# Seven block products for eight in part of the down projection of a decoder layer

## The chip, the cores and the metric

The kernel runs on one core of one Trainium2 chip. The metric is the device time of one execution in microseconds. It is given as the median of several runs; one further execution was recorded by the hardware profiler, and all views of the profile are of that one.

## The reference

One decoder layer on 256 tokens of width 1024, in float32: a combined input projection, pooling and attention heads, an output projection, cross-attention into 256 memory tokens, and a dense gated feed-forward block, each followed by a LayerNorm with a scaled residual. The change touches the last block:

```python
def swiglu(h, w_gate, w_up, w_down):
    return (jax.nn.silu(h @ w_gate) * (h @ w_up)) @ w_down
...
        h = layer_norm(DEEPNORM_ALPHA * h + swiglu(h, w_gate[l], w_up[l], w_down[l]),
                       ln3_g[l], ln3_b[l])
```

`w_gate` and `w_up` are 1024x2816, `w_down` is 2816x1024, and `DEEPNORM_ALPHA` is the fourth root of 2.

## The kernel before

Matrix products are done in a split form. Each float32 operand is kept as a high part, rounded to the format that TensorE reads (`hi`), and the remainder (`lo`). A product of two such operands is three matmuls, high by high, high by low and low by high, which `three` issues (lines 258 to 260). For a weight the high part is a cast on ScalarE (line 96) and the low part a subtraction on VectorE (line 98). `split` (lines 321 and 322) does the same for activations.

All large weights go through one `Stream` in a fixed order. It keeps 7 buffers for raw weights as they arrive by DMA on SyncE's queue (line 80) and 8 buffers each for high and low parts. A tile of the stream has 128 partitions of 1024 columns. `prepare` makes the parts of the next tiles and then fetches further raw ones. While TensorE uses tile i, the tiles up to i + 8 are prepared, each as soon as the tile eight places back has been used. Engines run their instructions in the order in which the program issues them; there is no reordering by a scheduler.

The feed-forward block has eleven chunks of 256 hidden channels (`NFC = 11`). For each chunk, `proj_both` computes gate and up in four PSUM banks: first for all eight blocks of 128 input channels the high weights against the high and low token parts side by side (32 matmuls of 512 columns, line 704), then the low weights against the high token parts (32 matmuls of 256 columns, line 710). Class `Gated` finishes a chunk during the next one: `add` joins the two halves of each bank (lines 840, 841), `multiply` applies silu and multiplies (lines 845, 846), and `split` makes the high and low parts of the gated activations, held transposed: 128 channels by 256 tokens, twice per chunk.

Down then multiplies the gated activations by `w_down`, 22 blocks of 128 rows, one tile of the stream each. A block of activations (128 channels by 128 tokens) is the stationary operand and 512 columns of weights move. `project` holds four accumulators, one for each pair of a token block and a half of the 1024 columns. It goes through the first 16 row blocks for all four. For the last 6 row blocks, which are all kept in the buffers, it goes accumulator by accumulator, the last in two pieces of 256 columns, so that the residual, the LayerNorm statistics (`Norm.add`) and the finish of a token block can begin while others are still computed. `Norm.finish`'s steps are done in `finish`: the statistics, the centring (line 618), the scaling (line 623) and the stores.

Of the kernel before, what the change touches and what calls it, by code (L numbers as in the profile page):

```python
# [8 lines left out]
F32 = mybir.dt.float32  # L9
F32R = mybir.dt.float32r  # L10
# [19 lines left out]
NEG = -3.0e38  # L30

RAW_BUFS, W_BUFS, AHEAD = 7, 8, 8
A8_BUFS = 9
PR_BUFS = 6
BUSY = 7


def r32(t):
    return t.bitcast(F32)


class Stream:


    def __init__(self, nc, pool):
        self.nc, self.pool = nc, pool
        self.src, self.raws, self.tiles, self.homes = [], [], [], []
        self.loads, self.splits = {}, {}
        self.used, self.held = 0, True
        self.pace, self.asked = 1, 0  # L50
        self.cuts, self.casts = {}, {}

    def add(self, src, parts=2):

        n = src.shape[1] // parts
        first = len(self.src)
        self.src += [src[:, i * n:(i + 1) * n, :] for i in range(parts)]
        return range(first, len(self.src))

    def before(self, number, load):  # L60

# [6 lines left out]
    def fetch(self, upto, queue):  # L68

        while len(self.raws) < min(upto, len(self.src)):  # L70
            i = len(self.raws)
            for load in self.loads.pop(i, []):
                load()
            src = self.src[i]
            if i < len(self.homes):
# [5 lines left out]
            self.raws.append(raw)  # L81

    def prepare(self, upto, eng=None):
        nc = self.nc
        while len(self.tiles) < min(upto, len(self.src)):
            i = len(self.tiles)
            src = self.src[i]
            for split in self.splits.pop(i, []):
                split()
            self.fetch(i + 1, nc.sync)  # L90
            raw = self.raws[i]
            hi = self.pool.tile(list(src.shape), F32R, tag="hi", name=f"w{i}h")
            lo = self.pool.tile(list(src.shape), F32R, tag="lo", name=f"w{i}l")
            for group in self.casts.get(i, [[slice(None)]]):
                for s in group:
                    nc.scalar.copy(hi[:, :, s], raw[:, :, s])  # L96
                s = slice(group[0].start, group[-1].stop)
                (eng or nc.vector).tensor_sub(lo[:, :, s], raw[:, :, s], r32(hi[:, :, s]))
            self.tiles.append((hi, lo))
            self.fetch(max(i + 1, len(self.homes)) + RAW_BUFS, nc.sync)  # L100

    def get(self, numbers, k):

# [24 lines left out]
def decoder_layer(  # L128
# [30 lines left out]
    def rows(w, k0, c0, nk=1, width=D):  # L159
        return ws.add(w[k0 * P:(k0 + nk) * P, c0:c0 + width].rearrange("(k p) n -> p k n", p=P), 1)  # L160
# [23 lines left out]
    c_dn = [rows(w_down, k, 0) for k in range(FB)]  # L184


    xt = ap.tile([P, T, D], F32, tag="a8", name="xt")
# [46 lines left out]
    ws.before(c_dn[4][0], load_norm("g", 3, ln3_g))  # L234
    ws.before(c_dn[6][0], load_norm("b", 3, ln3_b))

    ident = cp.tile([P, P], F32, name="ident")
    make_identity(nc, ident)
# [16 lines left out]
    def three(ps, w, y, start, stop, part=False):  # L255

        (wa, wb), (ya, yb) = w, y
        nc.tensor.matmul(ps, wa, ya, start=start, stop=False, skip_group_check=part)  # L258
        nc.tensor.matmul(ps, wa, yb, start=False, stop=False, skip_group_check=part)  # L259
        nc.tensor.matmul(ps, wb, ya, start=False, stop=stop, skip_group_check=part)  # L260

    def pair(hl, *ix):
        return hl[0][ix], hl[1][ix]
# [48 lines left out]
    def run(gen, n=None):  # L312

        while n is None or n > 0:
            if next(gen, gen) is gen:
                return False
            n = None if n is None else n - 1
        return True

    def split(h, l, ps):  # L320
        nc.scalar.copy(h, ps)  # L321
        nc.vector.tensor_sub(l, ps, r32(h))  # L322
# [265 lines left out]
    class Norm:  # L588
# [105 lines left out]
    oT = (a8("oTh", F32R), a8("oTl", F32R))  # L694
    xqT, xpr, xpt = {}, {}, {}

    def proj_both(pss, numbers, yT):

        for k in range(KD):
            hi, _ = ws.get(numbers, k)
            for b, ps in enumerate(pss):
                nc.tensor.matmul(ps, hi[:, b * P:(b + 1) * P], yT.both(k), start=k == 0, stop=False,  # L704
                                 skip_group_check=True)
            yield
        for k in range(KD):
            _, lo = ws.parts_of(numbers, k)
            for b, ps in enumerate(pss):
                nc.tensor.matmul(ps[:, S:], lo[:, b * P:(b + 1) * P], yT.pair(k)[0], start=False,  # L710
                                 stop=k == KD - 1, skip_group_check=True)
            ws.done(numbers, k)
            if not ws.held:
                ws.prepare(min(ws.used + AHEAD, len(ws.tiles) + 1))
            yield

    def do_xq(h):

# [55 lines left out]
    xattend(0)  # L774
    run(xq[3])

    h2 = ap.tile([P, T, D], F32, tag="a8", name="h2")
    xo = project(c_xo, lambda k: (oT[0][:, k], oT[1][:, k]), 4)
    xattend(1)
# [8 lines left out]
    xattend(3)  # L788


    h2T = Both("h2T")
    gT = [(a8(f"gTh{i}", F32R), a8(f"gTl{i}", F32R)) for i in range(3)]
    norm = Norm(2, h1[:, 0, :], h2[:, 0, :])
    for half in HALVES:
        norm.add(*half, until(xo)[1])
# [14 lines left out]
    run(xo)  # L810


    sg0 = sp.tile([P, T, CW], F32, name="sg", tag="pr", bufs=PR_BUFS)

    def gated_row(t, ps):
# [5 lines left out]
    def gated_t():  # L821
        pt = bank("pgt").rearrange("p (f t) -> p f t", f=2)
        for t in range(T):
            for f in range(2):
                nc.tensor.transpose(pt[:, f, t * P:(t + 1) * P], sg0[:, t, f * P:(f + 1) * P], ident)
        split(gT[0][0][:, 0:2, :], gT[0][1][:, 0:2, :], pt)

    class Gated:

# [16 lines left out]
            nc.vector.tensor_mul(gate, gate, up)  # L846
# [36 lines left out]
    pieces = PIECES[:3] + ((1, 512, 768), (1, 768, D))  # L883
    dn = project(c_dn, lambda k: (gT[k // KD][0][:, k % KD], gT[k // KD][1][:, k % KD]), 6, pieces)
    run(dn, 2)
    left.multiply()
    run(dn, 2)
    left.split()
    def finish(norm, t):
# [10 lines left out]
    norm = Norm(3, h2[:, 0, :])  # L900
    for half in HALVES:
        acc = until(dn)[1]
        for c in (0, 256):
            norm.add(half[0] + c, half[0] + c + 256, acc[:, c:c + 256])
    finish(norm, 0)

    norm = Norm(3, h2[:, 1, :])
    left = until(dn)[1]
    for c in (0, 256):
        norm.add(c, c + 256, left[:, c:c + 256])  # L910
    right = until(dn)[1]
    norm.sum(768, D, right[:, 256:])
    norm.add(512, 768, right[:, :256])
    last = until(dn)[1]
    nc.vector.tensor_add(norm.r[:, 768:], norm.r[:, 768:], last)
    norm.measure(768, D)
    finish(norm, 1)
    run(dn)
# [47 lines left out]
```

## Time and profile before

| | |
|---|---|
| median of 3 runs | 383.17 us (382.63 to 383.43) |
| profiled execution | 382.6 us, of which its span is 380.8 us |
| granted TensorE clock, mean | 0.995 |
| busy in the span: TensorE matmul | 372.1 us, 2172 instructions |
| VectorE | 262.9 us, 401 instructions |
| ScalarE | 187.8 us, 297 instructions |
| gate/up, chunks 1 to 10 | from 201.29 us, the last chunk from 301.72 us |
| down | from 312.67 us |
| last add of down's result | at 372.97 us |

The span runs from the first to the last instruction; the time of a run also holds what lies around it. A row of a timeline gives the start, the duration, the engine, the line of the kernel, the operation with what it writes and reads, and in square brackets the engine's idle time before it with what ended that. Matmuls overlap, so the step from one to the next is shorter than the duration shown.

### The profile page before, as it was taken

Reading aid. Unit: us, or ns where it says so; the run is one execution under the profiler, and the core shown is the slowest. Engines: PE = TensorE matmul, PEld = TensorE weight load, DVE = VectorE, ACT = ScalarE, POOL = GpSimd, SP = SyncE. Lnnn points to the kernel's source line nnn. Section 1 sums busy time; section 2 is a strip of 40 time slices with the busy share of each in tenths; the row PEclk is TensorE's granted clock in tenths of the full one; section 3 lists DMA queues with packets and bytes.
Section 4 is the critical chain, followed back from the end, with each engine's and each line's share of the span. In section 5 each row is a group of like instructions: output and inputs, shape, how many; then the busy total and the mean of one; then the engine's idle time right before and its main releaser. Section 6 shows DMA issues by size and latency. Waiting matters only on the chain.

```text
span 380.8 us, 5667 instructions
## 1 busy us (share of the span) xinstructions
PE 372.1 (98%) x2172; PEld 326.9 (86%) x2172; DVE 262.9 (69%) x401; ACT 187.8 (49%) x297; POOL 20.4 (5%) x31
## 2 busy tenths in 40 slices
PE   9999999999999999999999999999999999999991
PEld 9997989898888898988888888888888888888881
DVE  6768889945699758865887866666676667354265
ACT  6656677544164636544155755656544564434000
POOL 1000036200110000000100000000000000000011
PEclk9999999999999999999999999999999999999998
DMA  8996674658409953343109855546664757520011
GB/s 283 412 413 246 226 271 148 220 185 291 154 2 350 355 177 113 119 158 110 55 9 333 308 170 173 173 171 213 220 219 159 275 179 275 178 99 0 0 50 62
DMA packets 21322, 71.93 MB, mean 189 GB/s; under 512 B 2480, under 2 KB 3504, under 8 KB 21168
## 3 DMA queue, kind: packets, MB, share of 16 engines
q1 hardware_dynamic: 20720, 71.05, 53.4%
q10 hardware_dynamic: 576, 0.52, 0.4%
q8 instruction: 17, 0.28, 0.3%
q14 instruction: 9, 0.07, 0.1%
HBM read 70.52 MB, written 1.05 MB: 188 GB/s over the span
## 4 chain that ended last, share of the span: by engine, by line
PE 98%; DVE 1%; POOLq 0%; DVEq 0%; issue 0%
PE pg L704 19%; PE pg L710 10%; PE acc L258 9%; PE acc L260 9%; PE acc L259 9%; PE pqk L392 6%; PE pxk L276 6%; PE pxq L704 4%; PE pu L276 3%; PE pxq L710 2%; PE xv L258 2%; PE xv L260 2%; PE xv L259 2%; PE xs L737 2%; PE pv L258 1%; PE pg L260 1%
## 5 line engine op out<-in xcount | busy, mean ns | idle before, releaser
L613 POOL TENSOR_TENSOR rs<-rs,mhalf 128x1 f32<-128x1 f32 x6 | 6.4, 1070 | 300.4 <-DVE rs L612 300.4
L840 ACT COPY sg<-pg 128x256 f32<-128x256 f32 x40 | 12.0, 386 | 20.8 <-PE pg L710 20.8
L845 ACT ACTIVATE sg<-sg 128x512 f32<-128x512 f32 x10 | 6.3, 632 | 16.4 <-DVE sg L841 16.4
L841 DVE TENSOR_TENSOR sg<-pg,sg 128x256 f32<-128x256 f32 x40 | 14.1, 417 | 0.0
L602 DVE SCALAR_TENSOR_TENSOR r<-h,acc 128x256 f32<-128x256 f32 (+1 forms) x12 | 5.9, 501 | 10.9 <-PE acc L260 10.9
L322 DVE TENSOR_TENSOR gTl<-sg,gTh 128x512 fp32r<-128x512 f32 x10 | 6.9, 692 | 6.2 <-ACT gTh L321 6.2
L428 ACT ACTIVATE xpr<-xs,mx 128x256 f32<-128x256 f32 x8 | 3.7, 470 | 14.3 <-DVE mx L439 14.3
L428 ACT ACTIVATE pr<-pr,mx 128x128 f32<-128x128 f32 (+1 forms) x16 | 7.1, 444 | 6.8 <-DVE mx L459 6.8
L321 ACT CAST gTh<-sg 128x512 fp32r<-128x512 f32 x10 | 6.2, 620 | 7.4 <-DVE sg L846 7.4
L605 DVE BATCH_NORM_STATS2 st<-r 128x6 f32<-128x512 f32 (+1 forms) x16 | 9.0, 561 | 0.5
L321 ACT CAST h2T<-tp 128x512 fp32r<-128x512 f32 x4 | 2.4, 588 | 13.2 <-PE tp L349 13.2
L618 DVE SCALAR_TENSOR_TENSOR r<-r,mv,g 128x512 f32<-128x512 f32 (+1 forms) x10 | 8.3, 851 | 0.0
L846 DVE TENSOR_TENSOR sg<-sg 128x512 f32<-128x512 f32 x10 | 6.9, 693 | 1.0
L503 POOL TENSOR_TENSOR win<-win 128x269 f32<-128x269 f32 (+2 forms) x6 | 6.5, 1082 | 0.5
L737 PE MATMUL xs<-xkTh,xq 128*128 128x256 f32 x32 | 6.4, 282 | 0.0
L503 POOL TENSOR_TENSOR win<-upad 128x271 f32<-128x271 f32 x4 | 3.5, 871 | 53.7 <-ACT upad L531 53.7
L433 DVE RECIPROCAL sm<-sm 128x2 f32<-128x2 f32 x12 | 2.0, 166 | 6.0 <-ACT xpr L428 4.5
L623 DVE SCALAR_TENSOR_TENSOR h<-r,rs,b 128x512 f32<-128x512 f32 x8 | 5.7, 747 | 0.5 <-DVE r L618 0.5
L321 ACT CAST h1T<-tp 128x512 fp32r<-128x512 f32 x4 | 2.4, 588 | 7.1 <-PE tp L349 7.1
L737 PEld LDWEIGHTS xs<-xkTh,xq 128*128 128x128 f32 x32 | 5.2, 191 | 0.2
L349 PEld LDWEIGHTS tp<-ident,h 128*128 128x128 f32 x32 | 3.9, 141 | 1.3 <-PE pg L260 0.5
L96 ACT CAST w39h<-w39r 128x1024 fp32r<-128x1024 f32 x1 | 1.1, 1056 | 7.8 <-PE acc L260 7.8
(997 smaller groups left out, 1322.2 us busy)
## 6 DMA issues: line engine op xcount, KB each, us to landing
g<-in_ln_g SPq DMA_DIRECT2D x3, 512.0 KB, 5.0
b<-in_ln_b SPq DMA_DIRECT2D x3, 512.0 KB, 7.1
wr<-in_w_qkv SPq DMA_DIRECT2D x5, 256.0 KB, 3.9
mr<-in_mem_t SPq DMA_DIRECT2D x1, 1024.0 KB, 12.0
xt<-in_x SPq DMA_DIRECT2D x1, 1024.0 KB, 9.0
xr<-in_x_t SPq DMA_DIRECT2D x3, 256.0 KB, 5.8
wr<-in_w_qkv SPq DMA_DIRECT2D x1, 512.0 KB, 5.6
w7r<-in_w_qkv SPq DMA_DIRECT2D x1, 512.0 KB, 6.6
```

The source lines that it names most:

```text
L258: nc.tensor.matmul(ps, wa, ya, start=start, stop=False, skip_group_check=part)
L259: nc.tensor.matmul(ps, wa, yb, start=False, stop=False, skip_group_check=part)
L260: nc.tensor.matmul(ps, wb, ya, start=False, stop=stop, skip_group_check=part)
L276: nc.tensor.matmul(pss[f], w[:, s], y, start=k == 0 and f == 0 and n == 0, stop=k == KD - 1 and n == 2, skip_group_check=True)
L321: nc.scalar.copy(h, ps)
L392: nc.tensor.matmul(qk[i][:, f, :], w[:, c * P:(c + 1) * P], y, start=k == 0 and f == 0 and w is hi and y is x_hi, stop=k == KD - 1 and w i ...
L428: nc.scalar.activation(dst[:, j, :], src[:, j, :], AF.Exp, bias=mx[:, j:j + 1], scale=sign, accum_out=sm[:, j:j + 1])
L704: nc.tensor.matmul(ps, hi[:, b * P:(b + 1) * P], yT.both(k), start=k == 0, stop=False, skip_group_check=True)
L710: nc.tensor.matmul(ps[:, S:], lo[:, b * P:(b + 1) * P], yT.pair(k)[0], start=False, stop=k == KD - 1, skip_group_check=True)
L737: nc.tensor.matmul(ps[:, t, :], q[:, kk, t * P:(t + 1) * P], k[:, 2 * h + kk], start=n == 0, stop=q is q_lo and kk == 1, skip_group_check= ...
L840: nc.scalar.copy(y[:, f, :], ps[:, S:])
L841: nc.vector.tensor_add(y[:, f, :], ps[:, :S], y[:, f, :])
```

## The change

A chunk of down is a product of a matrix of 2x2 token and channel blocks (A) with a matrix of 2x2 weight blocks (B): the two token blocks by the two blocks of 128 channels, and the two blocks of 128 channels by the two halves of 512 columns. Before, this takes eight block products. For chunks 1 to 6 the change uses seven products of sums and differences of blocks (Winograd's form of Strassen's scheme), each still three matmuls of 512 columns. The remaining five chunks keep eight.

The sums of activations are formed on VectorE in `Gated.split`: four additions or subtractions of 128x128, followed by a second cast and subtraction for their high and low parts. The sums of weights are formed on VectorE in the raw buffers, in place, in `prepare_pair`. A paired chunk is three tiles of the stream instead of two: the lower row block together with one half of the upper one (which goes to a buffer of its own, `own`), then the upper buffer after it was overwritten by two differences, then the lower buffer after it was overwritten in turn. Two raw transfers serve the three.

The seven products accumulate over the six chunks in PSUM, in eight banks with the one that only unpaired chunks use. Unpaired chunks add to four of these banks. Three of the banks hold sums shared between quarters of the result. After the first eight chunks the shared banks are joined to the residual on VectorE. Then the last three chunks (8, 9 and 10, unpaired) are computed quarter by quarter as before, and each quarter is added.

The order of chunks in down becomes 1, 0, 2, 3, 4, 7, 5, 6, 8, 9, 10. In the last two chunks of gate/up, `proj_both` alternates between high and low weights in groups of two blocks instead of eight, and no tile is prepared in the last step of the last chunk. There are 11 instead of 9 large activation buffers; the room comes from a scratch area that is cut to 256 bytes.

```diff
-A8_BUFS = 9
+A8_BUFS = 11
+DOWN = (1, 0, 2, 3, 4, 7, 5, 6, 8, 9, 10)
+SEVEN = (1, 2, 3, 4, 5, 6)
+LAST = DOWN[-3:]
...
+    def prepare_pair(self, i, hi, lo):
+        nc = self.nc
+        first, step = self.pairs[i]
+        self.fetch(first + 2, nc.sync)
+        x, y = self.raws[first], self.raws[first + 1]
+        h = x.shape[2] // 2
+        (x1, x2), (y1, y2) = [(a[:, :, :h], a[:, :, h:]) for a in (x, y)]
+        sub = nc.vector.tensor_sub
+        if step == 0:
+            own = self.corner[first] = self.own(first)
+            nc.scalar.copy(own[:, 0:1, :], x1)
+            nc.scalar.copy(hi, y)
+            sub(own[:, 1:2, :], x1, r32(own[:, 0:1, :]))
+            sub(x1, x2, x1)
+            sub(x2, y2, x2)
+            sub(lo, y, r32(hi))
+        elif step == 1:
+            nc.scalar.copy(hi, x)
+            sub(y2, y2, x1)
+            sub(y1, y1, y2)
+            sub(lo, x, r32(hi))
+        else:
+            nc.scalar.copy(hi, y)
+            sub(lo, y, r32(hi))
...
+    def next(self):
+
+        if not self.held:
+            self.prepare(min(self.used + AHEAD, len(self.tiles) + 1))
...
+    def proj_both(pss, numbers, yT, group=KD):
+        for k0 in range(0, KD, group):
+            for k in range(k0, k0 + group):
+                hi, _ = ws.get(numbers, k)
...
+            for k in range(k0, k0 + group):
+                _, lo = ws.parts_of(numbers, k)
...
+                ws.done(numbers, k)
+                ws.next()
+                yield
...
         def split(self):
-            i, f = divmod(2 * self.c, KD)
-            split(gT[i][0][:, f:f + 2, :], gT[i][1][:, f:f + 2, :], self.sums[0])
+            gated_parts(self.c)
+            hi, lo = gT[self.c]
+            q = self.sums[0].rearrange("p f (t s) -> p (f t) s", t=T)
+            split(hi[:, 0:4], lo[:, 0:4], q)
+            if self.c in SEVEN:
+                a11, a21, a12, a22 = [q[:, i] for i in range(4)]
+                sums = sp.tile([P, 4, P], F32, name="sg", tag="pr", bufs=PR_BUFS)
+                s1, s2, s3, s4 = [sums[:, i] for i in range(4)]
+                nc.vector.tensor_add(s1, a21, a22)
+                nc.vector.tensor_sub(s3, a11, a21)
+                nc.vector.tensor_sub(s2, s1, a11)
+                nc.vector.tensor_sub(s4, a12, s2)
+                split(hi[:, 4:8], lo[:, 4:8], sums)
...
-        gu = proj_both(pss, c_gu[c], h2T)
+        gu = proj_both(pss, c_gu[c], h2T, KD if c < NFC - 2 else 2)
...
+        if c == NFC - 1:
+            run(gu, 2 * KD - 5)
+            ws.held = True
         run(gu)
         left = Gated(c, pss)
         left.add()
+    ws.held = False
+    ws.next()
...
+    m = {n: accbank(f"m{n}") for n in (1, 2, 3, 5)}
+    m |= {n: bank(f"m{n}") for n in (7, 6, 4, 0)}
...
+    def seven(c):
+        first = c_dn[c][0]
+        plan = (((1, 0, None), (2, 2, 0), (3, 7, 1)), ((5, 4, 0), (7, 6, 1)), ((6, 5, 1), (4, 3, 0)))
+        for i, products in enumerate(plan):
+            ws.prepare(first + i + 1)
+            hi, lo = ws.tiles[first + i]
+            for n, form, half in products:
...
+                into(n, pair(gT[c], ALL, form), w)
+                yield
+            ws.used += 1
+            ws.next()
...
+    def pieces():
+        for n, c0, c1 in ((2, 0, 512), (3, 0, 512), (4, 0, 512), (0, 0, 256), (0, 256, 512)):
...
+    dn = down()
     run(dn, 2)
     left.multiply()
-    run(dn, 2)
+    run(dn, 1)
     left.split()
+    run(dn)
+
+    lower, upper = slice(0, 512), slice(512, D)
+    norms = [Norm(3, h2[:, t, :]) for t in range(T)]
...
+    m1, u2, u3 = [shared_sum(name) for name in ("m1", "u2", "u3")]
+    nc.scalar.copy(m1, m[1])
+    with_residual(0, lower, m[1])
+    nc.vector.tensor_add(u2, m[6], m1)
+    with_residual(0, upper, m[5])
+    nc.vector.tensor_add(norms[0].r[:, upper], norms[0].r[:, upper], u2)
+    nc.vector.tensor_add(u3, m[7], u2)
+    with_residual(1, upper, m[5])
+    nc.vector.tensor_add(norms[1].r[:, upper], norms[1].r[:, upper], u3)
+    with_residual(1, lower, u3)
+    dn = pieces()
...
-    nc = bacc.Bacc("TRN2", target_bir_lowering=False, num_devices=1)
+    nc = bacc.Bacc("TRN2", target_bir_lowering=False, num_devices=1, dynamic_dma_scratch_size=256)
```

More of the change, by code (lines that the diff above doesn't have):

```diff
@@ L46, in __init__ @@
         self.nc, self.pool = nc, pool
+        self.pairs, self.corner = {}, {}
         self.src, self.raws, self.tiles, self.homes = [], [], [], []
@@ L58, in add, with add_pair @@
         return range(first, len(self.src))
+    def add_pair(self, upper, lower):
+        first = len(self.src)
+        self.src += [upper, lower, None]
+        for i in range(3):
+            self.pairs[first + i] = (first, i)
+        return range(first, first + 3)
     def before(self, number, load):
@@ L74, in fetch @@
             src = self.src[i]
+            if src is None:
+                self.raws.append(None)
+                continue
             if i < len(self.homes):
@@ L81, in fetch, with fetch_ahead @@
             self.raws.append(raw)
+    def fetch_ahead(self):
+        while len(self.raws) < len(self.src):
+            i, done = len(self.raws), len(self.tiles)
+            waiting = [j for j in range(len(self.homes), i)
+                       if self.src[j] is not None and j + (j in self.pairs) >= done]
+            if len(waiting) >= RAW_BUFS:
+                break
+            self.fetch(i + 1, self.nc.sync)
+    def prepare_pair(self, i, hi, lo):
[22 more added lines that the diff above has]
+            sub(lo, y, r32(hi))
     def prepare(self, upto, eng=None):
@@ L91, in prepare @@
             raw = self.raws[i]
-            hi = self.pool.tile(list(src.shape), F32R, tag="hi", name=f"w{i}h")
-            lo = self.pool.tile(list(src.shape), F32R, tag="lo", name=f"w{i}l")
+            shape = list((self.src[i - 1] if src is None else src).shape)
+            hi = self.pool.tile(shape, F32R, tag="hi", name=f"w{i}h")
+            lo = self.pool.tile(shape, F32R, tag="lo", name=f"w{i}l")
+            if i in self.pairs:
+                self.prepare_pair(i, hi, lo)
+                self.tiles.append((hi, lo))
+                self.fetch_ahead()
+                continue
             for group in self.casts.get(i, [[slice(None)]]):
@@ L183, in decoder_layer @@
     c_gu = [ws.add(w_gu[c], 4) for c in range(NFC)]
-    c_dn = [rows(w_down, k, 0) for k in range(FB)]
+    c_dn = {}
+    for c in DOWN:
+        tiles = [w_down[k * P:(k + 1) * P, :].rearrange("(k p) n -> p k n", p=P) for k in (2 * c, 2 * c + 1)]
+        c_dn[c] = ws.add_pair(*tiles) if c in SEVEN else [ws.add(w, 1)[0] for w in tiles]
+    ws.own = lambda i: sp.tile([P, 2, 512], F32R, tag="pair", bufs=3, name=f"w{i}c")
     xt = ap.tile([P, T, D], F32, tag="a8", name="xt")
@@ L233, in decoder_layer @@
     ws.before(c_xo[0][0], load_norm("b", 2, ln2_b))
-    ws.before(c_dn[4][0], load_norm("g", 3, ln3_g))
-    ws.before(c_dn[6][0], load_norm("b", 3, ln3_b))
+    ws.before(c_dn[DOWN[2]][0], load_norm("g", 3, ln3_g))
+    ws.before(c_dn[DOWN[3]][0], load_norm("b", 3, ln3_b))
     ident = cp.tile([P, P], F32, name="ident")
@@ L695, in decoder_layer @@
     xqT, xpr, xpt = {}, {}, {}
[L697 to L715, printed above, removed]
+    def proj_both(pss, numbers, yT, group=KD):
+        for k0 in range(0, KD, group):
+            for k in range(k0, k0 + group):
+                hi, _ = ws.get(numbers, k)
+                for b, ps in enumerate(pss):
+                    nc.tensor.matmul(ps, hi[:, b * P:(b + 1) * P], yT.both(k), start=k == 0, stop=False,
+                                     skip_group_check=True)
+                yield
+            for k in range(k0, k0 + group):
+                _, lo = ws.parts_of(numbers, k)
+                for b, ps in enumerate(pss):
+                    nc.tensor.matmul(ps[:, S:], lo[:, b * P:(b + 1) * P], yT.pair(k)[0], start=False,
+                                     stop=k == KD - 1, skip_group_check=True)
+                ws.done(numbers, k)
+                ws.next()
+                yield
     def do_xq(h):
@@ L775, in decoder_layer @@
     run(xq[3])
+    h2T = Both("h2T")
     h2 = ap.tile([P, T, D], F32, tag="a8", name="h2")
@@ L788, in decoder_layer @@
     xattend(3)
-    h2T = Both("h2T")
-    gT = [(a8(f"gTh{i}", F32R), a8(f"gTl{i}", F32R)) for i in range(3)]
     norm = Norm(2, h1[:, 0, :], h2[:, 0, :])
@@ L810, in decoder_layer, with gated_parts, gated_pair @@
     run(xo)
+    gT, shared = {}, {}
+    def gated_parts(c):
+        if c in SEVEN:
+            t = ap.tile([P, 2, 8, P], F32R, tag="a8", name=f"g{c}")
+            gT[c] = t[:, 0], t[:, 1]
+            return
+        i, j = divmod([c for c in sorted(DOWN) if c not in SEVEN].index(c), 2)
+        if j == 0:
+            shared[i] = ap.tile([P, 2, 8, P], F32R, tag="a8", name=f"go{i}")
+        gT[c] = tuple(shared[i][:, n, 4 * j:4 * j + 4] for n in range(2))
+    def gated_pair(c, k, t):
+        return pair(gT[c], ALL, 2 * k + t)
     sg0 = sp.tile([P, T, CW], F32, name="sg", tag="pr", bufs=PR_BUFS)
@@ L825, in gated_t @@
                 nc.tensor.transpose(pt[:, f, t * P:(t + 1) * P], sg0[:, t, f * P:(f + 1) * P], ident)
-        split(gT[0][0][:, 0:2, :], gT[0][1][:, 0:2, :], pt)
+        gated_parts(0)
+        split(gT[0][0], gT[0][1], pt.rearrange("p f (t s) -> p (f t) s", t=T))
     class Gated:
@@ L877, in decoder_layer, with into @@
         left.add()
+    ws.held = False
+    ws.next()
     def store(t, y, c0, c1, queue=nc.sync):
         queue.dma_start(out[t * P:(t + 1) * P, c0:c1], y[:, c0:c1])
-    pieces = PIECES[:3] + ((1, 512, 768), (1, 768, D))
-    dn = project(c_dn, lambda k: (gT[k // KD][0][:, k % KD], gT[k // KD][1][:, k % KD]), 6, pieces)
+    m = {n: accbank(f"m{n}") for n in (1, 2, 3, 5)}
+    m |= {n: bank(f"m{n}") for n in (7, 6, 4, 0)}
+    begun = set()
+    def into(n, y, w, cols=ALL, ps=None):
+        three((m[n] if ps is None else ps)[:, cols], y, w, n not in begun, True, True)
+        begun.add(n)
@@ new lines, in seven @@
+    def seven(c):
[5 more added lines that the diff above has]
+            for n, form, half in products:
+                if half is None:
+                    own = ws.corner[first]
+                    w = own[:, 0], own[:, 1]
+                else:
+                    w = tuple(a[:, 0, half * 512:(half + 1) * 512] for a in (hi, lo))
+                into(n, pair(gT[c], ALL, form), w)
+                yield
+            ws.used += 1
+            ws.next()
@@ new lines, in decoder_layer, with eight @@
+    QUARTERS = {2: (0, 0, 512), 3: (0, 512, D), 4: (1, 0, 512), 0: (1, 512, D)}
+    def eight(c):
+        for k, number in enumerate(c_dn[c]):
+            ws.prepare(number + 1)
+            hi, lo = ws.tiles[number]
+            for n, (t, c0, c1) in QUARTERS.items():
+                into(n, gated_pair(c, k, t), (hi[:, 0, c0:c1], lo[:, 0, c0:c1]))
+            ws.used += 1
+            ws.next()
+            yield
+    def pieces():
+        for n, c0, c1 in ((2, 0, 512), (3, 0, 512), (4, 0, 512), (0, 0, 256), (0, 256, 512)):
+            t, first, _ = QUARTERS[n]
+            ps = accbank("acc") if c0 else m[n]
+            for c in LAST:
+                for k, number in enumerate(c_dn[c]):
+                    ws.prepare(number + 1)
+                    w = pair(ws.tiles[number], ALL, 0, slice(first + c0, first + c1))
+                    if c0:
+                        three(ps[:, :c1 - c0], gated_pair(c, k, t), w, (c, k) == (LAST[0], 0), True, True)
+                    else:
+                        into(n, gated_pair(c, k, t), w, slice(c0, c1))
+                    yield
+            yield ps[:, :c1 - c0] if c0 else ps
@@ L885, in decoder_layer, with down, with_residual, shared_sum @@
+    def down():
+        for c in DOWN[:-len(LAST)]:
+            yield from (seven if c in SEVEN else eight)(c)
+    dn = down()
     run(dn, 2)
     left.multiply()
-    run(dn, 2)
+    run(dn, 1)
     left.split()
+    run(dn)
+    lower, upper = slice(0, 512), slice(512, D)
+    norms = [Norm(3, h2[:, t, :]) for t in range(T)]
+    def with_residual(t, s, y):
+        nc.vector.scalar_tensor_tensor(norms[t].r[:, s], h2[:, t, s], ALPHA, y, op0=OP.mult, op1=OP.add)
+    def shared_sum(name):
+        return sp.tile([P, 512], F32, name=name, tag="pr", bufs=PR_BUFS)
@@ L898, in finish, with add @@
         store(t, norm.r, 768, D)
-    norm = Norm(3, h2[:, 0, :])
+    def add(norm, c0, c1, acc):
+        nc.vector.tensor_add(norm.r[:, c0:c1], acc, norm.r[:, c0:c1])
+    norm = norms[0]
     for half in HALVES:
-        acc = until(dn)[1]
+        acc = until(dn)
         for c in (0, 256):
-            norm.add(half[0] + c, half[0] + c + 256, acc[:, c:c + 256])
+            add(norm, half[0] + c, half[0] + c + 256, acc[:, c:c + 256])
+            norm.measure(half[0] + c, half[0] + c + 256)
     finish(norm, 0)
-    norm = Norm(3, h2[:, 1, :])
-    left = until(dn)[1]
+    norm = norms[1]
+    acc = until(dn)
     for c in (0, 256):
[L910 to L915, printed above, removed]
+        add(norm, c, c + 256, acc[:, c:c + 256])
+        norm.measure(c, c + 256)
+    acc = until(dn)
+    add(norm, 768, D, acc[:, 256:])
+    add(norm, 512, 768, acc[:, :256])
+    norm.measure(512, 768)
+    add(norm, 768, D, until(dn))
     norm.measure(768, D)
```

2 lines of the change are left out of this document (1 added, 1 removed).

## The prediction

> **What bounds the kernel now.** I read the page's totals and chain first, then the chain in order of time around the start of down, then the timeline of each engine there, and last the windows.
>
> ```profile
> PE 372.1 (98%) x2172; PEld 326.9 (86%) x2172; DVE 262.9 (69%) x401; ACT 187.8 (49%) x297; POOL 20.4 (5%) x31
> PE 98%; DVE 1%; POOLq 0%; DVEq 0%; issue 0%
> 301.72 7.28 PE pg L704 x32
> 309.00 3.83 PE pg L710 x32
> 312.67 0.40 PE L258 MATMUL acc<-w103h,gTh 128*128 128x512 f32 x1
> 315.42 0.39 PE L258 MATMUL acc<-w104h,gTh 128*128 128x512 f32 x1
> 318.14 0.39 PE L258 MATMUL acc<-w105h,gTh 128*128 128x512 f32 x1
> 370.37 0.28 PE L259 MATMUL acc<-w124l,gTh 128*128 128x256 f32 x1
> 372.65 0.28 PE L260 MATMUL acc<-w124h,gTl 128*128 128x256 f32 x1
> 372.97 0.42 DVE L915 TENSOR_TENSOR r<-r,acc 128x256 f32<-128x256 f32 x1 [0.38 <-PE acc L260]
> ```
>
> TensorE is the chain. The rows w104h and w105h are 12 products apart: 2.72 us, so 0.2267 us for each 128x512 product (the 0.39 includes latency). The two rows of w124 are 19 products of 256 columns apart: 0.12 us each. Down has 16 x 12 + 6 x 9 = 246 wide products and 6 x 6 = 36 narrow ones: 246 x 0.2267 + 36 x 0.12 = 60.1 us after 312.67, which is where the last one stands. I call 312.67 T0 and count from it. The last add, L915, starts at 60.3, 0.2 us behind the last product; until it, down runs at TensorE's pace.
>
> **What TensorE loses.** Six chunks give seven products of three matmuls each for eight: 6 x 3 = 18 wide matmuls less, 18 x 0.2267 = 4.08 us. The last add could then start at 56.2. [...] Writing the last two gate/up chunks in groups of two keeps their 64 matmuls. 32 wide ones took 7.28 us where 32 x 0.2267 is 7.25, so a return from narrow to wide costs at most 0.03 us; there are six more: 0.16 us on the path. Since weights of those chunks are released tile by tile, nothing later is held up by this. Each of the formed operands is an ordinary 128x128 stationary or 128x512 moving block, so the price of a product stays.
>
> **What VectorE gains.** This decides the result. Its rows:
>
> ```profile
> 163.09 0.68 DVE L322 TENSOR_TENSOR oTl<-xo,oTh 128x512 fp32r<-128x512 f32 x1
> 163.69 0.68 DVE L322 TENSOR_TENSOR xst<-xpt,xst 128x512 fp32r<-128x512 f32 x1
> 187.28 0.68 DVE L602 SCALAR_TENSOR_TENSOR r<-h,acc 128x512 f32<-128x512 f32 x1
> 187.99 0.69 DVE L605 BATCH_NORM_STATS2 st<-r 128x6 f32<-128x512 f32 x1
> 178.97 1.23 DVE L98 TENSOR_TENSOR w62l<-w62r,w62h 128x1024 fp32r<-128x1024 f32 x1 [0.26 <-ACT w62h L96]
> 295.14 1.04 ACT L96 CAST w103h<-w103r 128x1024 fp32r<-128x1024 f32 x1
> 298.93 1.23 DVE L98 TENSOR_TENSOR w103l<-w103r,w103h 128x1024 fp32r<-128x1024 f32 x1 [2.98 <-PE pg L710]
> 301.21 1.22 DVE L98 TENSOR_TENSOR w105l<-w105r,w105h 128x1024 fp32r<-128x1024 f32 x1
> 302.35 1.22 DVE L98 TENSOR_TENSOR w106l<-w106r,w106h 128x1024 fp32r<-128x1024 f32 x1
> 303.48 1.41 DVE L841 TENSOR_TENSOR sg<-pg,sg 128x256 f32<-128x256 f32 x4
> 305.00 0.69 DVE L846 TENSOR_TENSOR sg<-sg 128x512 f32<-128x512 f32 x1
> 306.38 0.69 DVE L322 TENSOR_TENSOR gTl<-sg,gTh 128x512 fp32r<-128x512 f32 x1 [0.69 <-ACT gTh L321]
> 349.35 1.22 DVE L98 TENSOR_TENSOR w123l<-w123r,w123h 128x1024 fp32r<-128x1024 f32 x1 [1.49 <-ACT w123h L96]
> core 0: us, PE busy (x) PEld busy (x) DVE busy (x) ACT busy (x) POOL busy (x), PEclk, DMA share, GB/s
> 290.40:301.50 11.10, 11.10 (x66) 9.83 (x65) 7.33 (x11) 6.24 (x11) 0.00 (x0) 1.00 0.77 285
> 312.60:340.00 27.40, 27.40 (x123) 22.70 (x123) 15.73 (x17) 11.62 (x15) 0.00 (x0) 1.00 0.62 209
> ```
>
> An operation that doesn't need the one before it starts early: 1024 columns every 1.14 us (w105l to w106l), 512 columns every 0.60 (163.09 to 163.69). One that reads its predecessor's result waits for it: 0.71 (187.28 to 187.99), which I take as 0.72, since 0.69 is the commoner duration. So a paired chunk of weights costs: tile one, three half-width subtractions and one full, 3 x 0.60 + 1.14 = 2.94; tile two, two half-width, the second a reader of the first, and one full, 1.32 + 1.14 = 2.46; tile three one full and a short wait for its cast, about 1.3. That is 6.7 us. If overwriting a block just read also waits, four steps cost 0.1 more: 7.1. I take 6.8. Two plain tiles cost 2.28 before. TensorE spends 21 x 0.2267 = 4.76 us on such a chunk, so VectorE is slower than TensorE there and lives on its lead of eight tiles.
>
> In gate/up a paired chunk also forms four 128x128 sums and splits them. No row has this size; between zero and the 0.35 of a 256-column add (1.41 / 4) I take the nearer upper end less a little, 0.25 each. With a cast and a subtraction the addition is 1.0 + 0.65 + 0.69 = 2.3 us, and the upper end 2.7. It lands in the 2.98 us that VectorE waits ahead of w103l, once a chunk, and the weights made behind it are needed a chunk (11.1 us) later. Cost: none; without this cover, up to 2.7 a chunk in six chunks. ScalarE's additions (3.6 us of casts per paired chunk, by 1.04 for 1024 columns) fit: it was busy 11.6 of 27.4.
>
> DMA moves the same 22 row blocks, two in 4.76 us instead of two in 5.44: 209 GB/s becomes 239, under the 285 of the other window. Seven raw buffers stay ahead, so I cost this at nothing; if they ran dry, TensorE would wait on SP's queue.
>
> **The ledger from T0.** In chunk 9 VectorE makes down's tiles 1 to 4 (2.94 + 2.46 + 1.3 + 1.14) beside 2.8 us of its old work (1.41 + 0.69 + 0.69): 10.6 of 11.1 us. In chunk 10 come a plain tile, then 2.94 and 2.46 of the next pair, each after a group has freed a buffer; these end about T0 + 0.8. Behind them are queued the four adds of chunk 10 (to 2.2), one full subtraction (3.4), the multiply, a 0.69 wait for the cast, and the split (5.5). Banks are free in time: the first product into one of chunk 10's banks is the fifth, at T0 + 2.7. From 5.5 on VectorE doesn't stop:
>
> two pairs, 13.6: 19.1; two plain tiles: 21.4; two pairs: 35.0; six plain tiles, 6.8: 41.8. TensorE reaches the last six tiles after 174 matmuls, at 39.45, and the last of them at 42.85. No wait for weights, but only 1 us to spare.
>
> Then eight 512-column operations that join the shared sums to the residual, 5.1 us: 46.9. These are new between the last weight and the first norm. The tail's prices:
>
> ```profile
> 364.58 0.42 DVE L602 SCALAR_TENSOR_TENSOR r<-h,acc 128x256 f32<-128x256 f32 x1 [2.42 <-PE acc L260]
> 366.28 0.26 DVE L610 BATCH_NORM_AGGREGATE mv<-st 128x2 f32<-128x24 f32 x1
> 369.82 0.41 DVE L602 SCALAR_TENSOR_TENSOR r<-h,acc 128x256 f32<-128x256 f32 x1
> 371.40 0.73 DVE L602 SCALAR_TENSOR_TENSOR r<-h,acc 128x256 f32<-128x256 f32 x2
> 372.16 0.43 DVE L605 BATCH_NORM_STATS2 st<-r 128x6 f32<-128x256 f32 x1
> ```
>
> A half row with its statistics takes 1.6 (369.82 to 371.40), the finish of a norm 3.54 (366.28 to 369.82), the next to last piece 1.2. First half row 48.5; second, whose products end at 47.8, 50.1; finish 53.6; third half row 55.2; next piece 56.4. The last add can start at 56.2 by TensorE and 56.4 by VectorE. With the dearer pairs (7.1 instead of 6.8, four times, and little losses ahead) it is 57.3. I take 56.6. What follows the last add is as before.
>
> Sum: 60.3 - 56.6 - 0.16 = 3.5 us gained. The profiled run took 382.6 us (span 380.8); this gives 379.1. The median of the runs is 383.17, 0.57 above the profiled one; as a median I forecast 379.6.
>
> **Rivals.** *VectorE's work is free.* If its operations overlap as the cheap rows do and the pair costs 6.6, TensorE alone sets the end: 60.3 - 56.2 - 0.16 = 3.9, a median of 379.2. This only edges the forecast.
>
> *The casts are late.* Each low part of a pair waits for a cast on ScalarE that itself waits for VectorE's in-place subtraction. Where casts weren't ahead, the row of w62l shows 0.26. Twelve such waits in four pairs are 3.1 us, of which 0.6 is counted above: the last add at 59.1, a gain of 1.0 and a median of 382.2. Against it: two operations (1.1 to 2.4 us) lie between the subtraction and the low part, longer than the 1.04 of the cast, except for the third tile.
>
> *VectorE doesn't overlap at all in chains of small dependent steps.* Then every 512-column operation costs 0.72 and every 1024-column one 1.25. A pair is 5 x 0.72 + 3 x 1.25 = 7.35, the backlog at the start, a pair and a half and eight older steps at these prices, ends at 6.7 instead of 5.5; four pairs, eight plain tiles: 6.7 + 29.4 + 10.0 = 46.1, past the 42.85 at which TensorE needs the last tile, so it waits 3.3 us in the first piece. Eight operations: 51.9; half rows at 1.8 each and the finish: 59.0; then 60.8 and, with the next piece at 1.3, 62.1. The last add is 1.8 us later than before: slower by 2.0, a median of 385.1. It decides from the point where VectorE is 3.5 us behind my ledger, 6% of 56.6. For it: formed sums overwrite their own inputs. Against it: w105l and w106l stand 1.14 apart at a duration of 1.22. [...]
>
> *The pairing removes nothing.* The loop order fixes 18 matmuls less; I see no way for it.
>
> **How the numbers follow.** Forecast with its own range (56.2 to 57.3 for the last add, medians of 379.2 to 380.3): 0.62, the free case included. Late casts, gains from 0.5 to 2.7: 0.2, of which 0.02 within measurement. No overlap, slower: 0.13. Ledger off by just the whole gain: 0.05. A difference of 0.2%, 0.8 us, is about what a measurement of this kernel can tell from no change. So faster 0.80, same 0.07, slower 0.13. The range runs from 378.8 (the free case less the spread of runs, 0.4) to 382.0, into the late casts.
>
> **What would show it.** After: 18 matmuls less; gate/up chunks still 11.1 us each with no wait on TensorE; down's VectorE without idle time from T0 to the end; paired chunks spaced 6.7 to 7.1 us on it, against 4.76 on TensorE; the last six tiles ready before TensorE asks; the last add waiting less than 0.4 us for TensorE. I am wrong if TensorE waits for a low part in the first pieces (no overlap), or VectorE shows a wait for a cast in front of each low part, or gate/up stretches.

## The result and the profile after

The changed kernel took 380.02 us in the median (379.81 to 380.66), the kernel before 383.08 us: a ratio of 0.9924, with a 95% interval of 0.9906 to 0.9941. In a second comparison, on the chip of the last experiments, it was 379.62 against 383.09 us, 0.9904 (0.9886 to 0.9921). Faster, then, by 3.1 and 3.5 us.

The profiled execution after took 380.66 us, with a span of 378.9. The page's totals:

```profile
PE 368.3 (97%) x2154; PEld 323.3 (85%) x2154; DVE 303.1 (80%) x475; ACT 200.3 (53%) x316; POOL 20.4 (5%) x31
```

TensorE has 18 matmuls less and VectorE is busy for 40 us more. The waits of TensorE show one thing that lies far ahead of the change, in the first ten microseconds:

```profile
PE pqk L462 <- ACT w2h L157: 1.0, 1, 1.0
```

TensorE waited 1.0 us for the third weight tile's cast. The view's one other row, 0.8 us at L432, stands in the kernel before as well (at its L362); no wait lies in gate/up or in down. The second profile of the changed kernel (experiment 10) lacks the wait for the cast, so it is no part of the change. All comparisons below therefore count from T0, the first matmul of down.

The chain in order of time, for gate/up's first long row, the end of gate/up and around the end of down:

```profile
202.54 7.26 PE pg L775 x32
...
308.62 1.84 PE pg L775 x8
310.46 0.95 PE pg L781 x8
...
348.68 0.24 PE m L330
348.95 0.53 ACT w125h L157
...
355.47 1.14 DVE w130l L159
356.60 0.60 DVE r L1061
```

Before, the chain ran on TensorE to the last add. Now it leaves TensorE at 348.68 and is ScalarE's and VectorE's work from there to the end: VectorE has become the engine that ends last. The casts in this chain did not hold VectorE up: its timeline shows no idle time in brackets from 319.18 until the first norm's wait for GpSimd (0.44 us, ahead of 366.91). The last two gate/up chunks alternate between 1.84 and 0.95 us of eight matmuls each: the regrouping.

The timeline of TensorE and VectorE in down:

```profile
314.04 0.40 PE L328 MATMUL m<-w103c,g 128*128 128x512 f32 x1
...
314.33 1.41 DVE L930 TENSOR_TENSOR sg<-pg,sg 128x256 f32<-128x256 f32 x4
...
319.18 0.69 DVE L125 TENSOR_TENSOR w111c<-w111r,w111c 128x512 fp32r<-128x512 f32 x1
319.90 0.69 DVE L126 TENSOR_TENSOR w111r<-w111r 128x512 f32<-128x512 f32 x1
320.63 0.69 DVE L127 TENSOR_TENSOR w111r<-w112r,w111r 128x512 f32<-128x512 f32 x1
321.24 1.22 DVE L128 TENSOR_TENSOR w111l<-w112r,w111h 128x1024 fp32r<-128x1024 f32 x1
322.49 0.69 DVE L131 TENSOR_TENSOR w112r<-w112r,w111r 128x512 f32<-128x512 f32 x1
323.21 0.69 DVE L132 TENSOR_TENSOR w112r<-w112r 128x512 f32<-128x512 f32 x1
323.82 1.22 DVE L133 TENSOR_TENSOR w112l<-w111r,w112h 128x1024 fp32r<-128x1024 f32 x1
325.10 1.23 DVE L136 TENSOR_TENSOR w113l<-w112r,w113h 128x1024 fp32r<-128x1024 f32 x1
326.25 0.69 DVE L125 TENSOR_TENSOR w114c<-w114r,w114c 128x512 fp32r<-128x512 f32 x1
...
355.39 1.21 DVE L159 TENSOR_TENSOR w130l<-w130r,w130h 128x1024 fp32r<-128x1024 f32 x1
356.52 0.68 DVE L1061 SCALAR_TENSOR_TENSOR r<-h,m 128x512 f32<-128x512 f32 x1
...
357.13 0.39 PE L329 MATMUL m<-w130l,go 128*128 128x512 f32 x1
...
369.94 0.28 PE L330 MATMUL acc<-w130h,go 128*128 128x256 f32 x1
371.06 0.41 DVE L1090 TENSOR_TENSOR r<-acc,r 128x256 f32<-128x256 f32 x1
```

T0 is 314.04. Counted from it, the last product starts at 55.9 and the last add at 57.02; before, the last add was at 60.3. One pair takes VectorE from 319.18 to 326.25, 7.07 us. The last low part (w130l) is done at 356.60, half a microsecond before TensorE uses it at 357.13. The last add shows no idle time in front of it: the last product stands 1.12 us ahead of it, where 0.32 was enough in the kernel before. So VectorE comes to it 0.8 us after TensorE would have allowed.

### The profile page after: what moved, and what is told of

The parts are those of the page before. It is cut to its first block, busy times and chain, and to the rows that moved or that the text cites. A ratio compares the mean times of both kernels' runs of the same rounds, so it can differ in the third digit from the quotient of the medians.

```text
span 378.9 us, 5741 instructions
## 1 busy us (share of the span) xinstructions
PE 368.3 (97%) x2154; PEld 323.3 (85%) x2154; DVE 303.1 (80%) x475; ACT 200.3 (53%) x316; POOL 20.4 (5%) x31
## 4 chain that ended last, share of the span: by engine, by line
PE 90%; DVE 5%; ACT 1%; DMA 1%; POOLq 0%; POOL 0%; SPq 0%; issue 0%; DVEq 0%; ACTq 0%
PE pg L775 19%; PE pg L781 10%; PE pxk L346 6%; PE pqk L462 5%; PE pxq L775 4%; PE acc L328 4%; PE acc L329 4%; PE acc L330 4%; PE pu L346 3%; PE m L330 3%; PE m L329 3%; PE m L328 3%; PE pxq L781 2%; PE xv L330 2%; PE xv L329 2%; PE xv L328 2%
## 5 line engine op out<-in xcount | busy, mean ns | idle before, releaser
L391 ACT CAST g<-sg 128x512 fp32r<-128x512 f32 x12 | 7.4, 621 | 15.1 <-DVE sg L949 10.1
L392 DVE TENSOR_TENSOR g<-sg,g 128x512 fp32r<-128x512 f32 x12 | 8.3, 693 | 8.2 <-ACT g L391 8.2
L391 ACT CAST xkTh<-pxk 128x512 fp32r<-128x512 f32 x4 | 2.4, 588 | 4.9 <-PE pxk L346 4.9
```

## The experiments

All times of the last add are counted from the first matmul of down in the same profile.

**1. No chunk paired.** This kernel has no sums to join and leaves the joining out; its last add overwrites, with an operation of the same shape, and so leaves out the first eight chunks' part of the last 256 columns of the second token block.

```diff
-SEVEN = (1, 2, 3, 4, 5, 6)
+SEVEN = ()
...
-        nc.vector.tensor_add(norm.r[:, c0:c1], acc, norm.r[:, c0:c1])
+        norm.sum(c0, c1, acc)
```

> No chunk is paired: all eleven take eight products, everything else (order of chunks, grouping of the last two gate/up chunks, buffers) stays as in the changed kernel. Theory (the gain is 18 matmuls at 0.2267 us, less what VectorE gives back): 264 matmuls again, the last add 60.3 us after down's first matmul, the time that of the kernel before plus the 0.12 us of the regrouping, 383.2. Rival (order, grouping or buffers bring part of the gain): clearly below 383, at 381.5 if half of it.

Measured: 382.85 us, a ratio of 0.9996 (0.9987 to 1.0005). The timeline:

```profile
313.02 0.40 PE L328 MATMUL m<-w103h,go 128*128 128x512 f32 x1
...
373.31 0.42 DVE L672 SCALAR_TENSOR_TENSOR r<-h,acc 128x256 f32<-128x256 f32 x1 [0.37 <-PE acc L330]
```

The last add is at 60.29, behind TensorE, as in the kernel before. Order, grouping and buffers bring nothing by themselves that this measurement could tell: the gain is that of the seven products.

**2. Five chunks paired.**

```diff
-SEVEN = (1, 2, 3, 4, 5, 6)
+SEVEN = (1, 2, 3, 4, 5)
```

> Chunks 1 to 5 are paired, chunk 6 takes eight products. Theory: VectorE has one pair less, 7.06 - 2.28 = 4.8 us less to do after down's start, so it is no longer late at the end; TensorE alone sets the end: 15 x 0.2267 = 3.40 less 0.12 of regrouping, 379.8, as fast as six pairs; the last add waits for TensorE. Rival (each pair brings its share, no lateness): five sixths of 3.06, 380.5.

Measured: 380.11 us, 0.9923 (0.9910 to 0.9935), within the spread of six pairs. The timeline:

```profile
313.53 0.40 PE L328 MATMUL m<-w103c,g 128*128 128x512 f32 x1
...
357.95 0.42 DVE L1090 TENSOR_TENSOR r<-m,r 128x256 f32<-128x256 f32 x1 [1.61 <-PE m L330]
...
370.42 0.42 DVE L1090 TENSOR_TENSOR r<-acc,r 128x256 f32<-128x256 f32 x1 [0.35 <-PE acc L330]
```

VectorE waits for TensorE again, at the first half row and at the last add. That stands at 56.89: 60.3 less 15 x 0.2267. Five pairs give what TensorE saves, whole; six save 0.68 more there and lose it on VectorE, with the last add at 57.02. The sixth pair is worth nothing as the kernel stands.

**3. One subtraction more in each pair.**

```diff
         else:
             nc.scalar.copy(hi, y)
             sub(lo, y, r32(hi))
+            sub(lo[:, :, :h], y1, r32(hi[:, :, :h]))
```

> Each pair does one 512-column subtraction more (it writes half of a low part a second time with the same values). Theory (VectorE sets the end): four pairs after down's start, 0.72 us each: the last add about 2.6 to 2.9 us later, TensorE waits about 2 us for the last weight tile, the time 382.7. Rival (TensorE sets the end and VectorE's work is hidden): no change, 380.0.

Measured: 383.68 us, 1.0020 (1.0010 to 1.0029). The timeline:

```profile
313.06 0.40 PE L329 MATMUL m<-w103c,g 128*128 128x512 f32 x1
...
314.08 1.41 DVE L931 TENSOR_TENSOR sg<-pg,sg 128x256 f32<-128x256 f32 x4
...
374.04 0.41 DVE L1091 TENSOR_TENSOR r<-acc,r 128x256 f32<-128x256 f32 x1
```

The last add is at 60.98, 3.96 later, and the whole gain is lost to 4 us of small subtractions. The direction was right, the size about a third too small, for two reasons that the expectation had missed. The third step of chunk 2's pair also lies after T0, so five operations count, 3.6 us. And the one in chunk 1's pair isn't absorbed either: the four adds start at T0 + 1.02 here and at T0 + 0.29 in the changed kernel. Of these 4.3 us, some 0.3 come back: the changed kernel's wait of 0.32 for the cast ahead of w110l is gone. So VectorE has no room left from chunk 9 of gate/up on. TensorE waits for weights here, as expected: 0.6 us for w123l and five times 0.2 for w126l to w130l, 1.6 in all.

**4. The last two gate/up chunks in one group.**

```diff
-        gu = proj_both(pss, c_gu[c], h2T, KD if c < NFC - 2 else 2)
+        gu = proj_both(pss, c_gu[c], h2T, KD)
```

> The last two gate/up chunks take the eight high blocks first and then the eight low ones, as in the kernel before. Theory: the buffers come free only in the last third of each chunk, VectorE idles there and starts down about 4.4 us later with its list, so TensorE waits about 4 us for the last weight tiles and the last add stands near 61.4: 384.4, slower than before the change. Rival (the grouping is not needed, the lead of eight tiles suffices): 379.9, the 0.12 us of regrouping better.

Measured: 383.21 us, 1.0006 (0.9997 to 1.0015). The timeline, then the windows around the wait in it (TensorE's busy time and count first, its granted clock in the third column from the right):

```profile
312.66 0.40 PE L328 MATMUL m<-w103c,g 128*128 128x512 f32 x1
...
316.96 1.41 DVE L930 TENSOR_TENSOR sg<-pg,sg 128x256 f32<-128x256 f32 x4
...
317.43 0.50 PE L328 MATMUL m<-w104h,g 128*128 128x512 f32 x1 [1.86 <-DVE sg L930]
...
319.04 0.63 PE L330 MATMUL m<-w105h,g 128*128 128x512 f32 x1
319.47 0.63 PE L328 MATMUL m<-w105h,g 128*128 128x512 f32 x1
...
372.32 0.28 PE L330 MATMUL acc<-w130h,go 128*128 128x256 f32 x1
373.30 0.41 DVE L1090 TENSOR_TENSOR r<-acc,r 128x256 f32<-128x256 f32 x1
```

```profile
315.40:317.40 2.00, 0.17 (x1) 0.00 (x0) 2.00 (x4) 1.22 (x2) 0.00 (x0) 1.00 0.00 0
...
318.20:321.60 3.40, 3.40 (x9) 2.61 (x8) 2.71 (x5) 1.64 (x4) 0.00 (x0) 0.51 0.74 237
```

The grouping is needed: without it VectorE starts on chunk 10's adds at T0 + 4.3 instead of 0.3, and the last add is at 60.64, not 57.0. But TensorE did not wait where the theory had it. The adds free the PSUM banks of chunk 10, and the fifth product of down needs the first of them. The prediction had put that at T0 + 2.7 and found it free in time; here it isn't. TensorE stands for 1.86 us, and its granted clock then drops to 0.51 for 3.4 us, with matmuls 0.43 us apart. No wait for a weight is left in this run's waits: TensorE, itself held up, asks for the last tiles later. What sets the end is still VectorE, as the theory had it: the last add has no idle time in front of it and stands 0.98 us behind the last product, where 0.32 would do. TensorE's stall and slower clock lie hidden behind VectorE's late list, with 0.7 us to spare.

**5. Independent operations between dependent ones.**

```diff
             sub(own[:, 1:2, :], x1, r32(own[:, 0:1, :]))
+            sub(lo[:, :, :h], y1, r32(hi[:, :, :h]))
             sub(x1, x2, x1)
+            sub(lo[:, :, h:], y2, r32(hi[:, :, h:]))
             sub(x2, y2, x2)
-            sub(lo, y, r32(hi))
```

> In the first step of each pair the low part is made in two halves, and they stand between the three in-place subtractions, so that no operation overwrites what the one just before it still reads. Theory (a VectorE operation waits for the one before it also where it only overwrites that one's input, and VectorE sets the end): two waits of 0.12 us less and one start of 0.06 us more per pair, 6.85 instead of 7.06 us, the last add 0.8 us earlier, 56.2 after down's first matmul, where TensorE takes over; 379.3. Rival (the waits are only between a writer and a reader): the pair stays at 7.1 us or gets 0.06 longer, the time unchanged.

Measured: 379.28 us, 0.9907 (0.9893 to 0.9920). The timeline of the cast wait in the first pair behind T0, of the next pair from its first operation to the tile behind it, and of the ends:

```profile
313.01 0.40 PE L329 MATMUL m<-w103c,g 128*128 128x512 f32 x1
...
319.02 0.69 DVE L126 TENSOR_TENSOR w111l<-w112r,w111h 128x512 fp32r<-128x512 f32 x1 [0.18 <-ACT w111h L124]
...
325.31 0.69 DVE L125 TENSOR_TENSOR w114c<-w114r,w114c 128x512 fp32r<-128x512 f32 x1
325.91 0.68 DVE L126 TENSOR_TENSOR w114l<-w115r,w114h 128x512 fp32r<-128x512 f32 x1
...
332.20 1.22 DVE L160 TENSOR_TENSOR w117l<-w117r,w117h 128x1024 fp32r<-128x1024 f32 x1
...
369.61 0.41 DVE L1091 TENSOR_TENSOR r<-acc,r 128x256 f32<-128x256 f32 x1
```

The operations now stand 0.60 apart where they stood 0.72 apart, and this pair takes 6.89 us instead of 7.07. So an operation that overwrites what its predecessor reads did wait, by 0.12 us. The last add is at 56.60, 0.4 earlier and not 0.8. In the first pair (from 318.15 to 325.31) the earlier low part now waits for its cast, and the pair takes 7.16, 0.09 longer than before. Each of the other three saves 0.18, not 0.21. The time can't tell this run from the changed kernel, since the intervals overlap; the positions in the profiles can.

**6 and 7. Part of the joining in the wait for GpSimd**, alone and together with experiment 5: three of the eight joining operations are issued behind the first norm's centring.

```diff
     nc.vector.tensor_add(u3, m[7], u2)
-    with_residual(1, upper, m[5])
-    nc.vector.tensor_add(norms[1].r[:, upper], norms[1].r[:, upper], u3)
-    with_residual(1, lower, u3)
...
         norm.centre(0, D)
+        if t == 0:
+            with_residual(1, upper, m[5])
+            with_residual(1, lower, u3)
+            nc.vector.tensor_add(norms[1].r[:, upper], norms[1].r[:, upper], u3)
         norm.scale(0, 512)
```

> Three of the eight operations that join shared sums to the residual, those of the second token block, are issued behind the first block's centring instead of ahead of the last pieces. Theory (VectorE sets the end, its only idle time in down is the 0.44 us wait for GpSimd's power): the last add 0.44 us earlier, 56.6 after down's first matmul; 379.6. Rival (TensorE or the order of the pieces sets the end): unchanged, or later since the operations now stand behind the first norm.

> Both of these together: VectorE could end 1.2 us earlier, TensorE allows 0.8: the last add waits for TensorE by about 0.35 us, at 56.2 after down's first matmul; the full price of 18 matmuls less the regrouping, 379.2. Rival (something else holds the end): no earlier than the better of the two alone.

Measured: 379.70 us, 0.9916 (0.9902 to 0.9929), and together 379.58, 0.9915 (0.9902 to 0.9929). Experiment 6's timeline:

```profile
313.17 0.40 PE L328 MATMUL m<-w103c,g 128*128 128x512 f32 x1
...
361.00 0.42 DVE L1091 TENSOR_TENSOR r<-m,r 128x256 f32<-128x256 f32 x1 [0.57 <-PE m L330]
...
370.22 0.41 DVE L1091 TENSOR_TENSOR r<-acc,r 128x256 f32<-128x256 f32 x1
```

The last add is at 57.05 in both. The 0.44 us were filled, but with three operations less ahead of the pieces VectorE comes too early to the second half row and waits 0.57 for TensorE there; the moved work then lies behind that wait. The theory failed by taking VectorE as one list without fixed points in it. Together with experiment 5, which brings VectorE earlier still, that wait only becomes longer (1.00 us), and the last add stands 0.45 behind that of experiment 5 alone; the times of the two can't be told apart.

**8 and 9. Two joining operations on GpSimd**, alone and together with experiment 5; **10**, the changed kernel beside them.

```diff
-    nc.vector.tensor_add(norms[0].r[:, upper], norms[0].r[:, upper], u2)
+    nc.gpsimd.tensor_add(norms[0].r[:, upper], norms[0].r[:, upper], u2)
...
-    nc.vector.tensor_add(norms[1].r[:, upper], norms[1].r[:, upper], u3)
+    nc.gpsimd.tensor_add(norms[1].r[:, upper], norms[1].r[:, upper], u3)
```

> Two of the eight operations that join the shared sums to the residual, the two whose operands all lie outside PSUM, are issued to GpSimd. Theory (VectorE sets the end by 0.8 us): they cost VectorE 0.72 us each with the wait behind them; without them TensorE sets the end, the last add at 56.2 after down's first matmul, 0.8 us earlier; 379.2. On GpSimd they take 1.2 to 3 us each by its rows of 270 columns (0.64 to 1.6), and have 4 us for the first and 9 for the second. Rival (GpSimd's reads hold VectorE up, or the joins come too late for the second half row): the last add no earlier than 57.0.

> The two joins on GpSimd and the low part of each pair's first step in two halves between the in-place subtractions. Theory: VectorE has room to spare, TensorE sets the end as with the joins alone: 56.2 after down's first matmul, 379.2, and the last add waits for TensorE by about 0.35 us. Rival (VectorE still sets the end): the two gains add, below 56.2 cannot be.

> The changed kernel itself once more, beside the two others on the same chip: last add 57.0 after down's first matmul, 380.0.

Measured, against the same runs of the kernel before: 378.99 us, 0.9888 (0.9867 to 0.9908) for the joins on GpSimd; 379.34, 0.9895 (0.9877 to 0.9913) with both; 379.62 for the changed kernel. Experiment 8's timeline, then the two ends of experiment 10's:

```profile
313.04 0.40 PE L328 MATMUL m<-w103c,g 128*128 128x512 f32 x1
...
357.54 1.29 POOL L1071 TENSOR_TENSOR r<-r,u 128x512 f32<-128x512 f32 x1 [165.47 <-DVE r L1061]
358.52 0.87 DVE L1061 SCALAR_TENSOR_TENSOR r<-h,u 128x512 f32<-128x512 f32 x1
358.79 1.76 POOL L1074 TENSOR_TENSOR r<-r,u 128x512 f32<-128x512 f32 x1
...
369.25 0.42 DVE L1090 TENSOR_TENSOR r<-acc,r 128x256 f32<-128x256 f32 x1 [0.29 <-PE acc L330]
```

```profile
312.97 0.40 PE L328 MATMUL m<-w103c,g 128*128 128x512 f32 x1
...
370.01 0.41 DVE L1090 TENSOR_TENSOR r<-acc,r 128x256 f32<-128x256 f32 x1
```

The last add waits for TensorE again and stands at 56.21, the 56.2 that 18 matmuls less allow. With experiment 5's order added it stands at 56.21 as well: ahead of the last add there is nothing more to have from VectorE. One VectorE operation that runs beside GpSimd takes 0.87 us instead of 0.68, in both runs, so the rival was not empty, but there was room for it. In experiment 10 the last add is at 57.04, against 57.02 in the first profile of the same kernel. The medians are 0.6 us apart where the traces say 0.8; their intervals overlap, and the positions in the profiles are what settles it. This version has the lowest median here.

## Why the prediction was right, and where its sizes were off

The sign, the mechanism and the range were right: 379.6 was forecast, 380.02 and 379.62 measured. From T0 the trace gives 60.3 - 57.02 - 0.12 = 3.16 us, for 3.5 forecast. That the second median meets the forecast to 0.02 us is luck: the last add, on which the forecast rests, was 0.4 us off.

- *18 matmuls at 0.2267 us*: shown. Experiments 1, 2 and 8 place the last add at 60.29, 56.89 and 56.21, each a count of matmuls times that price. One reading was off without touching the difference: 60.1 is where the products end; the last one starts at 59.98, 0.32 ahead of the add.
- *Regrouping*: 0.16 forecast; gate/up from its first long row to down takes 111.50 instead of 111.38, 0.12.
- *Sums in gate/up are hidden*: shown. The rows of a middle chunk, before and then after:

```profile
254.48 1.23 DVE L98 TENSOR_TENSOR w87l<-w87r,w87h 128x1024 fp32r<-128x1024 f32 x1 [2.98 <-PE pg L710]
```

```profile
255.73 1.22 DVE L159 TENSOR_TENSOR w87l<-w87r,w87h 128x1024 fp32r<-128x1024 f32 x1 [0.67 <-PE pg L781]
```

2.31 us of the idle time are used, for 2.3 forecast.

- *A pair costs 6.8*: this term was mis-sized. It is 7.07, almost the dearer of the two prices that were worked out (7.1): a write over a block just read waited like a read of a result, 0.72 us from start to start (319.18 to 319.90, and 322.49 to 323.21 for the read) instead of 0.60. Three steps of a pair are such writes (not four), about 0.12 us each. Over four pairs that is 1.1 us more than at 6.8. An error the other way hid part of it: VectorE entered its list 0.4 us earlier than forecast (5.1 instead of 5.5). So the last low part came at 42.5 instead of 41.8, and the last add at 57.02 instead of 56.6. The prediction's upper bound of 57.3 is also less than its own terms give: 56.4 and four times 0.3 are 57.6.
- *Weights are ready in time*: they were, by 0.5 us instead of 1.
- *The rival of no overlap* did not come about, since half-width operations without a dependency stand 0.60 apart (325.31 to 325.91 in experiment 5). Dependent ones, overwriting included, stand 0.72 apart (319.18 to 319.90 in the changed kernel). The margin was small: in experiment 3 a list 4 us longer lost the whole gain.
- *Late casts*: only the third tile of a pair waits, as forecast: 0.14 us (w113l at 325.10, 1.28 behind its predecessor), and once 0.32 (w110l, at T0 + 2.02). This and the forecast wait of 0.69 ahead of chunk 10's split are VectorE's idle time between T0 and its list.

## What to carry to other kernels

A saving on the busiest engine is worth its full price only until the engine that pays for it becomes the last; work out both lists to the end of the stage, from the same starting point, and compare where they end. Here a sixth pair saved 0.68 us on TensorE and cost all of it on VectorE, which two small operations on GpSimd, idle for 165 us until then, gave back (experiment 8, last add at 56.21). When moving work on an engine that runs it in the order of issue, as VectorE did here (in experiment 6 the three moved operations follow the centring), look for the fixed points at which it waits for another: time moved across one can be lost, as in the 0.57 us that VectorE waited there for TensorE.

## What the runs showed of the hardware

In the profiled execution of experiment 4, a TensorE gap of 1.86 us (ahead of 317.43) was followed, from 318.2 on, by 3.4 us at a granted clock of 0.51, with 512-column matmuls 0.43 us apart (319.04 to 319.47) instead of 0.227; by an estimate from these numbers (0.49 of 3.4, 1.7 us) TensorE lost about as much again as the gap lasted. Not every execution seems to have had such a drop; this too is an estimate, from the mean clocks. The drop takes 0.004 off the mean clock (0.49 of 3.4 in 381 us), no run here is above 0.997, and four of experiment 4's ten runs have 0.995, too much for a run with such a drop in it. They took 383.03 to 383.47 us, the other six 382.93 to 383.62: by this the drop does not set that kernel's time.

A 512-column float32 addition took GpSimd 1.29 and 1.76 us in experiment 8, about two to two and a half times VectorE's 0.69, and still helped, since no wait for it shows in front of VectorE's additions that follow.
